# A hybrid encoder layer on one core: query scaling in the scan's first level, eleven low weight parts made and stored beside the last input pairs, and the order of steps around them

## The chip, the cores and the metric

The kernel runs on one core of a Trainium2 chip. The metric is the device time of one execution in microseconds (us). Before the change three executions took 1735.74, 1736.81 and 1737.69 us; the median is 1736.81 us. A profile of one more execution, which took 1736.41 us, is the source of every duration below.

## The reference

For one sequence of 1024 positions and 1024 channels, the layer computes

```python
h = rmsnorm(x)
glu_in, q, v, z_f, z_b, og, g_a, g_b = split(h @ w_in)        # 1024 x 8192
a = pointwise(silu(layernorm(dwconv31(glu(glu_in)))))
o = scan(q, k_f, v, f_f) + flip(scan(flip(q), flip(k_b), flip(v), flip(f_b)))   # 8 heads of 128
b = (rmsnorm(o) * silu(og)) @ o_w
x = x + (sigmoid(g_a) * a + sigmoid(g_b) * b) @ w_out
h2 = rmsnorm(x)
x = x + (silu(dwconv3(h2 @ w_gate)) * (h2 @ w_up)) @ w_down
out = rmsnorm(x)
```

`scan` is a gated linear recurrence per head, S_t = diag(f_t) S_(t-1) + k_t v_t', o_t = S_t' q_t, with the forget gate f and the key k = (1 - lb) sigmoid(-z), where lb is a learned bound per channel and direction. Everything is float32.

## The kernel before, in words

**Dense products.** Every weight tile is cut into a high part (an ACT cast, L125) and a low part (a VectorE subtract, L125), and every product is three TensorE matmuls (L149, L150, L151: low activation times high weight and so on) of 128x128 by 128x512. The program writes TensorE's order by hand: a job yields after each *piece*, and `fill(n)` on a stream makes the next n pieces of it (fractions are owed). What VectorE, ACT, GpSimd (POOL) and the DMA queues do is placed around that by a scheduler; `pin` holds an instruction where it was written.

**Input pairs.** The columns of `w_in` are taken two tiles at a time, 19 pairs (`in_pair`), each by seven products of half-size blocks (84 dense matmuls). Of each pair VectorE makes weight sums and low parts (`wq`, `wp`, and for some pairs the sums `sw` and `wr` at L298; for the other pairs POOL's accumulating DMAs make those sums), and combines the products as they end (`ev`, L800). TensorE reuses a few PSUM banks here (`tr`, `mm`, `sc`), so a later product waits until the `ev` of an earlier one has read its bank.

**Conv stage, about 100 to 340 us.** `conv_steps` makes the 31 taps of four channel tiles on VectorE (L1036, L1039: 128x1024 multiply-add, 124 of them); after each tap `s_pairs.fill(CONV_FILL)` puts in 1.67 pieces of the input pairs.

**LayerNorm stage, about 400 to 470 us.** For each half of the sequence: the mean by a matmul with `ones_m` (L1065), subtraction (L1067), squares on ACT, their sum (`tm`, L1051 and L1053) into a matmul (L611), the scale, then normalise, SiLU and split (L1077 to L1082). Pieces of the last pairs lie between: six after the mean, five after the sum of squares, twelve at the end of a half.

**Scan stage, about 510 to 865 us.** There are 16 half-heads. `scan_base` (L1220) prepares one: scaled keys, products of queries and forget gates, and running products of gates by doubling (L1144); its fourth step has TensorE's first group of small matmuls (called S here: `sc<-q,A` and `sc<-A,A`, L1195). `scan_levels` (L1280) goes on with two more levels (called O: `ob<-A,A`, L1195), sixteen zero matmuls that clear a bank (L1302), `blocks(32)` and `blocks(64)` (L1281, called B32 and B64); `scan_states` has the transposes of the keys (L1320) and the state updates (L1329); `scan_outputs` (L1370) follows a head later, fed by `pending`. Between these steps `between` puts in 1.77 pieces of dense filler (`std_job` columns of `w_in`), one step of the next half-head's base, and one step of pending outputs. The filler's low parts are made by VectorE as each tile arrives.

**End.** The last dense jobs leave the final rows (`final_evac`, `turn_out`, `finish`): transposes at L1890 and the scale on ACT at L1926.

## Time and profile before

| what | value |
|---|---|
| profiled execution, its own time | 1736.41 us |
| its span in the profile | 1734.3 us (2.1 us lie outside it) |
| median of three unprofiled runs | 1736.81 us |
| TensorE (PE) busy | 1709.2 us, 99% |
| VectorE (DVE) busy | 1255.9 us, 72% |
| ScalarE (ACT) busy | 830.3 us, 48% |
| GpSimd (POOL) busy | 170.4 us, 10% |
| granted TensorE clock | 0.998 |

A busy share counts from the start of a matmul to its modelled end, so overlapped matmuls hide small gaps: for TensorE the distance from one start to the next says more. Where TensorE waits, the table of waits names the instruction that waited, the engine and line that released it, the sum, the number of such waits and the longest.

### The profile page before, as it was taken

How to read it: one execution, taken by the hardware profiler on the slowest of the kernel's cores; microseconds unless marked ns; L12 is line 12 of the kernel's file. 1: busy time of each engine (PE TensorE's matmuls, PEld its weight loads, DVE VectorE, ACT ScalarE, POOL GpSimd, SP SyncE). 2: the span in 40 equal slices, each digit the busy share in tenths (PEclk: the TensorE clock that was granted, in tenths of full speed). 3: DMA queues.
4: the chain of work that ended last, by engine and by line, in shares of the span. 5: the costliest groups of instructions: out<-in, count | busy, mean ns of one | idle time of the engine just before them, and what ended most of it. 6: DMA issues, size and time to landing. Idle time of an engine off the chain costs nothing.

```text
span 1734.3 us, 30669 instructions
## 1 busy us (share of the span) xinstructions
PE 1709.2 (99%) x11902; PEld 1415.0 (82%) x11902; DVE 1255.9 (72%) x1937; ACT 830.3 (48%) x1544; POOL 170.4 (10%) x185
## 2 busy tenths in 40 slices
PE   8999999999999999999999999999999999999997
PEld 6878888888788888888878888888888888888787
DVE  5599999746778888888557466667767776657865
ACT  7444443334566777776442245444434433542334
POOL 2211111100000000000000002011111111000110
PEclk9999999999999999999999999999999999999999
DMA  8768888854673444435579466568777776783842
GB/s 288 239 167 184 193 194 193 197 167 154 207 230 104 131 126 132 127 115 192 175 248 333 147 207 205 146 148 170 158 170 160 180 172 153 229 267 107 205 91 98
DMA packets 343751, 308.27 MB, mean 178 GB/s; under 512 B 25262, under 2 KB 255798, under 8 KB 343606
## 3 DMA queue, kind: packets, MB, share of 16 engines
q1 hardware_dynamic: 289590, 267.51, 48.7%
q0 software_dynamic: 44800, 37.76, 15.2%
q10 hardware_dynamic: 9216, 1.05, 0.4%
q8 instruction: 93, 1.52, 0.4%
q14 instruction: 52, 0.43, 0.1%
HBM read 201.40 MB, written 87.03 MB: 166 GB/s over the span
## 4 chain that ended last, share of the span: by engine, by line
PE 44%; DMA 2%; DVE 2%; ACT 1%; issue 1%; SPq 0%; POOL 0%; POOLq 0%; ACTq 0%; DVEq 0%
PE mm L151 10%; PE mm L150 10%; PE mm L149 10%; PE sc L149 3%; PE sc L150 3%; PE sc L151 3%; PE tr L149 1%; PE tr L150 1%; PE tr L151 1%; DMA tm<-d_bm 1%; DVE hx L125 0%; DMA wr<-in_ffn_w_down_dram 0%; DMA wr<-wr 0%; DMA d_gc<-ft 0%; DVE wp L125 0%
## 5 line engine op out<-in xcount | busy, mean ns | idle before, releaser
L149 PE MATMUL mm<-hx,wp 128*128 128x512 f32 x1068 | 428.0, 401 | 3.3 <-ACT tm L851 2.1
L151 PE MATMUL mm<-hx,wp 128*128 128x512 f32 x1068 | 418.1, 391 | 0.9 <-DVE wp L125 0.8
L150 PE MATMUL mm<-hx,wp 128*128 128x512 f32 x1068 | 416.9, 390 | 0.3 <-DVE hx L125 0.2
L125 ACT CAST wp<-wr 128x1024 fp32r<-128x1024 f32 (+2 forms) x147 | 147.2, 1002 | 259.2 <-PE mm L150 119.5
L151 PEld LDWEIGHTS mm<-hx,wp 128*128 128x128 f32 x1068 | 200.9, 188 | 46.3 <-DVE wp L125 3.4
L149 PEld LDWEIGHTS mm<-hx,wp 128*128 128x128 f32 x1068 | 200.8, 188 | 46.1 <-ACT tm L851 2.6
L150 PEld LDWEIGHTS mm<-hx,wp 128*128 128x128 f32 x1068 | 201.2, 188 | 41.3 <-DVE hx L125 1.6
L125 DVE TENSOR_TENSOR wp<-wr,wp 128x1024 fp32r<-128x1024 f32 (+2 forms) x145 | 169.3, 1168 | 68.5 <-ACT wp L125 67.9
L1039 DVE SCALAR_TENSOR_TENSOR acc<-gl,v_b,acc 128x1024 f32<-128x1024 f32 x120 | 148.9, 1277 | 0.4
L1144 DVE TENSOR_TENSOR qF<-qF,tb 128x512 f32<-128x512 f32 x96 | 65.0, 684 | 20.8 <-ACT A L1176 20.7
L440 ACT COPY su<-mm 128x512 f32<-128x512 f32 x82 | 47.7, 582 | 66.2 <-PE mm L151 66.2
L149 PE MATMUL tr<-hx,wp 128*128 128x512 f32 x180 | 70.5, 392 | 0.0
L125 ACT CAST wq<-sw 128x1024 fp32r<-128x1024 f32 x41 | 43.2, 1053 | 56.3 <-PE mm L150 40.5
L151 PE MATMUL tr<-hx,wp 128*128 128x512 f32 x180 | 70.1, 389 | 0.0
L150 PE MATMUL tr<-hx,wp 128*128 128x512 f32 x180 | 70.0, 389 | 0.0
L1636 DVE SCALAR_TENSOR_TENSOR tm<-gp,v_a,tm 128x512 f32<-128x512 f32 x88 | 65.9, 749 | 3.9 <-ACT tm L1634 2.0
L1144 DVE TENSOR_TENSOR kG<-kG,tb 128x512 f32<-128x512 f32 x96 | 65.1, 684 | 3.7 <-PE sc L1281 3.7
L149 PE MATMUL mm<-hy,wp 128*128 128x512 f32 x164 | 64.2, 391 | 0.0
L149 PE MATMUL sc<-hy,wq 128*128 128x512 f32 x164 | 64.2, 391 | 0.0
L151 PE MATMUL sc<-hy,wq 128*128 128x512 f32 x164 | 63.8, 389 | 0.0
L150 PE MATMUL mm<-hy,wp 128*128 128x512 f32 x164 | 63.8, 389 | 0.0
L150 PE MATMUL sc<-hy,wq 128*128 128x512 f32 x164 | 63.8, 389 | 0.0
(372 smaller groups left out, 3609.9 us busy)
## 6 DMA issues: line engine op xcount, KB each, us to landing
wr<-in_w_in_dram SPq DMA_DIRECT2D x48, 512.0 KB
wr<-in_ffn_w_up_dram SPq DMA_DIRECT2D x22, 512.0 KB
sw<-in_w_in_dram SPq DMA_DIRECT2D x38, 256.0 KB
d_g<-ft SPq DMA_DIRECT2D x38, 256.0 KB
sw<-in_ffn_w_up_dram SPq DMA_DIRECT2D x38, 256.0 KB
sw<-in_ffn_w_up_dram POOLq DMA_DIRECT2D x19, 512.0 KB, 8.1
wr<-sw POOLq DMA_DIRECT2D x32, 256.0 KB, 3.8
wr<-wr POOLq DMA_DIRECT2D x32, 256.0 KB, 4.1
```

What stands on the lines that cost most here:

```text
L125: parts = A.copy(hi, src), eng.tensor_tensor(lo, src, hi.bitcast(F32), op=ALU.subtract)
L149: T.matmul(acc, whi[:, k, :], ahi, start=first, stop=False, skip_group_check=again)
L150: T.matmul(acc, whi[:, k, :], alo, start=False, stop=False, skip_group_check=again)
L151: T.matmul(acc, wlo[:, k, :], ahi, start=False, stop=last, skip_group_check=again)
L440: A.copy(t, acc)
L1039: V.scalar_tensor_tensor(acc, g[:, k : k + S], tap(k), acc, op0=ALU.mult, op1=ALU.add)
L1144: V.tensor_tensor(o, a, b, op=op)
L1636: V.scalar_tensor_tensor(c, g[:, o + k : o + k + H], vec("fdw", k * NF + j), c, op0=ALU.mult, op1=ALU.add,)
```

## The change

It has seven parts.

1. `CONV_FILL` goes from 1.67 to 1.6, so 124 taps carry 198 pieces instead of 207.
2. `first` holds from pair 12 on instead of 14: pairs 12 and 13 make their weight sums on VectorE and no longer by POOL's accumulating DMAs.
3. `low_part`: for eleven filler tiles of the scan (the fourth to the fourteenth), POOL loads the raw tile (512 KB) in the LayerNorm stage, five pieces later ACT casts it and VectorE subtracts (both pinned), and two pieces later POOL stores the result. One tile is begun every five pieces. In the scan these tiles' low parts are loaded by the SP queue; VectorE makes none for them.
4. In the LayerNorm stage the twelve pieces at the end of a half become 1.5 pieces after each of the four channel tiles and 1.5 at the end.
5. In `scan_base` the keys are no longer scaled in place; the scale goes into the sum of keys and into the queries' first products (two 128x512 and four 128x256 instructions in place of three 128x512 sums and products and two scalings).
6. In `scan_levels` the zero matmuls and B32 come straight behind O, and two fills instead of one lie before B64. The next base is begun two steps earlier (its first step falls into the half-head before), and in `between` the base's step comes behind `pending`.
7. At the end the transposes of the final rows come a few pieces later.

TensorE gets the same matmuls in another order (7757 rows before and after). VectorE has 1853 rows before and 1843 after, ACT 1396 and 1389, POOL 184 and 200, SP 891 and 904.

**VectorE, conv stage, third pair** (`acc` a tap; `ev` from `tr`, `mm`, `sc` the combining of the products; `wq` from `sw` and from `w` two low parts). Before:

```order
L800 TENSOR_TENSOR ev_1873<-tr_1818,su_1833 128x512
L1039 SCALAR_TENSOR_TENSOR acc_1532<-gl_473,v_b,acc_1532 128x1024
L1039 SCALAR_TENSOR_TENSOR acc_2057<-gl_464,v_b,acc_2057 128x1024
L1039 SCALAR_TENSOR_TENSOR acc_1532<-gl_473,v_b,acc_1532 128x1024
L1039 SCALAR_TENSOR_TENSOR acc_2057<-gl_464,v_b,acc_2057 128x1024
L1039 SCALAR_TENSOR_TENSOR acc_1532<-gl_473,v_b,acc_1532 128x1024
L800 TENSOR_TENSOR ev_1921<-su_1906,mm_1817 128x512
L125 TENSOR_TENSOR wq_1863<-sw_1850,wq_1862 128x1024
L1039 SCALAR_TENSOR_TENSOR acc_1532<-gl_473,v_b,acc_1532 128x1024
L125 TENSOR_TENSOR wq_1870<-w_302_1860,wq_1870 128x512
```

After, the same place:

```order
L1045 SCALAR_TENSOR_TENSOR acc_1543<-gl_484,v_b,acc_1543 128x1024
L806 TENSOR_TENSOR ev_1885<-tr_1830,su_1845 128x512
L1045 SCALAR_TENSOR_TENSOR acc_1543<-gl_484,v_b,acc_1543 128x1024
L1045 SCALAR_TENSOR_TENSOR acc_2054<-gl_475,v_b,acc_2054 128x1024
L1045 SCALAR_TENSOR_TENSOR acc_1543<-gl_484,v_b,acc_1543 128x1024
L1045 SCALAR_TENSOR_TENSOR acc_2054<-gl_475,v_b,acc_2054 128x1024
L1045 SCALAR_TENSOR_TENSOR acc_1543<-gl_484,v_b,acc_1543 128x1024
L125 TENSOR_TENSOR wq_1875<-sw_1862,wq_1874 128x1024
L1045 SCALAR_TENSOR_TENSOR acc_1543<-gl_484,v_b,acc_1543 128x1024
L125 TENSOR_TENSOR wq_1882<-w_302_1872,wq_1882 128x512
L806 TENSOR_TENSOR ev_1933<-su_1918,mm_1829 128x512
```

One tap moved ahead of the first `ev`, and both low parts and a tap moved ahead of the `ev` that frees the bank `mm`.

**VectorE, LayerNorm, second half**, from the subtraction of the mean to the last `tm` before the sum of squares (`sw` and `wr` at L298 are weight sums). Before:

```order
L1067 SCALAR_TENSOR_TENSOR cx_3969<-ob_4022,cx_3969 128x512 x2
L1067 SCALAR_TENSOR_TENSOR cx_3972<-ob_4022,cx_3972 128x512 x2
L298 TENSOR_TENSOR wr_4032<-wr_4032,sw_4034 128x512
L1051 TENSOR_TENSOR tm_4102<-tm_4102,tm_4103 128x512
L298 TENSOR_TENSOR wr_4032<-wr_4032 128x512
L1053 TENSOR_TENSOR tm_4102<-tm_4102,tm_4104 128x512
L1053 TENSOR_TENSOR tm_4102<-tm_4102,tm_4105 128x512
```

After (`lw` at L1076 is a new low part; the first of its subtractions of `cx`, the same row with `cx_3925`, is left out above the first row):

```order
L1095 SCALAR_TENSOR_TENSOR cx_3928<-ob_4007,cx_3928 128x512 x2
L125 TENSOR_TENSOR wq_3954<-sw_3939,wq_3953 128x1024
L806 TENSOR_TENSOR ev_4028<-su_3999,mm_3896 128x512
L806 TENSOR_TENSOR ev_4044<-sc_3898,su_3984 128x512
L125 TENSOR_TENSOR wq_3961<-w_621_3951,wq_3961 128x512
L1076 TENSOR_TENSOR lw_3975<-lw_3885,lw_3975 128x1024
L1057 TENSOR_TENSOR tm_4076<-tm_4076,tm_4077 128x512
L303 TENSOR_TENSOR sw_4120<-sw_4120,sw_4123 128x1024
L1076 TENSOR_TENSOR lw_4025<-lw_3973,lw_4025 128x1024
L125 TENSOR_TENSOR wp_3958<-wr_3937,wp_3957 128x1024
L1059 TENSOR_TENSOR tm_4076<-tm_4076,tm_4078 128x512
L1059 TENSOR_TENSOR tm_4076<-tm_4076,tm_4079 128x512
```

Between the mean and the last `tm` two wr rows became two `lw`, two `wq`, two `ev`, a `wp` and the sum `sw`, which needs a load.

**TensorE, scan, first half-head**: O (`ob<-A,A`), the zero matmuls (`none`, sixteen of them, the first shown) and dense matmuls (`hx,wp`). Before:

```order
L151 MATMUL mm_4640<-hx_4311,wp_4450 128x512
L1195 MATMUL ob_4674<-A_4577,A_4575 32x32 x16
L1195 MATMUL ob_4674<-A_4623,A_4621 32x32 x16
L149 MATMUL mm_4640<-hx_4317,wp_4449 128x512
L150 MATMUL mm_4640<-hx_4318,wp_4449 128x512
L151 MATMUL mm_4640<-hx_4317,wp_4450 128x512
L149 MATMUL mm_4640<-hx_4323,wp_4449 128x512
L150 MATMUL mm_4640<-hx_4324,wp_4449 128x512
L151 MATMUL mm_4640<-hx_4323,wp_4450 128x512
L1302 LDWEIGHTS none
L1302 MATMUL sc_4730<-none 32x32
```

After, up to the first zero matmul, and then from the last one on (`qF,kG` 32x32 is B32, `ident,tm` the transposes of v):

```order
L151 MATMUL mm_4722<-hx_4392,wp_4532 128x512
L1228 MATMUL ob_4772<-A_4659,A_4657 32x32 x16
L1228 MATMUL ob_4772<-A_4705,A_4703 32x32 x16
L1336 LDWEIGHTS none
L1336 MATMUL sc_4805<-none 32x32
```

```order
L1336 MATMUL sc_4805<-none 32x32
L1318 MATMUL sc_4805<-qF_4504,kG_4417 32x32 x16
L149 MATMUL mm_4722<-hx_4398,wp_4531 128x512
L150 MATMUL mm_4722<-hx_4399,wp_4531 128x512
L151 MATMUL mm_4722<-hx_4398,wp_4532 128x512
L149 MATMUL mm_4722<-hx_4404,wp_4531 128x512
L150 MATMUL mm_4722<-hx_4405,wp_4531 128x512
L151 MATMUL mm_4722<-hx_4404,wp_4532 128x512
L1509 MATMUL tr_4862<-ident,tm_4770 128x128 x4
```

The six dense matmuls moved from between O and the zero matmuls to behind B32, ahead of the transposes.

The diff, cut to its core:

```diff
@@ -19,16 +19,16 @@
 TAIL = ((1, 2), (1, 1), (2, 4), (2, 3))
-CONV_FILL = 1.67
+CONV_FILL = 1.6
 NPAIRS = 19
+STAGE_FROM, STAGED, STAGE_STEP = 3, 11, 5
 LN_FILL = 6
-LN_LAST = 12
+LN_STEP = 1.5
 GLU_FIRST = 4
...
 GLU_LATE = 17
-BASE_STEPS = 1
 ALIGN = 128
...
 EPS = 1e-6

@@ -248,12 +248,17 @@
-    def std_job(src, nk, acts, evac, halves=(0, 1), step=2):
+    def std_job(src, nk, acts, evac, halves=(0, 1), step=2, low=None):
...
             raw = raw_w(src, nk)
-            return split(w_page(nk), w_page(nk), raw, V)
+            if low is None:
+                return split(w_page(nk), w_page(nk), raw, V)
+            hi, lo = w_page(nk), w_page(nk)
+            nc.sync.dma_start(lo.bitcast(F32), low)
+            A.copy(hi, raw)
+            return hi, lo
...
             for half in halves:

@@ -563,6 +568,7 @@
     d_z = scratch("d_z", 2, NH, 2)
+    d_lo = [dp.tile([P, ND, P], F32, name=f"d_lo_{i}") for i in range(STAGED)]
     d_bm = scratch("d_bm", NH, 2)
...
     d_xt = [[d_x0[:, :, k, :], scratch(f"d_xt_{k}")] for k in range(ND)]

@@ -838,7 +844,7 @@
             lambda e, *quadrant: evs[e](*quadrant),
-            first=n == 0 or n >= 14,
+            first=n == 0 or n >= 12,
             columns=2,
...

@@ -1053,6 +1059,28 @@
+    def low_part(i):
+        src = in_cols(todo[2 * NPAIRS + STAGE_FROM + i][0])
+        def w_tile(dt):
+            return gp0.tile([P, ND, P], dt, tag="gl", name=nm("lw"), bufs=NCW)
+        def fetch_raw():
+            raw = w_tile(F32)
+            G.dma_start(raw, src)
+            later(5, lambda: take(raw))
+        def take(raw):
+            lo = w_tile(F32R)
+            pin(A.copy(lo, raw))
+            pin(V.tensor_tensor(lo, raw, lo.bitcast(F32), op=ALU.subtract))
+            later(2, lambda: G.dma_start(d_lo[i], lo.bitcast(F32)))
+        later(1 + STAGE_STEP * i, fetch_raw)
+    for i in range(STAGED):
+        low_part(i)
     for half in range(2):
...
         for j in range(NCW):

@@ -1077,17 +1105,22 @@
             A.activation(xn, xn, AF.Silu)
+            s_pairs.fill(LN_STEP)
             both = gp0.tile([P, 2, H], F32R, tag="gl", name=nm("ch"), bufs=NCW)
...
                 nc.sync.dma_start(dst, part.bitcast(F32))
-        s_pairs.fill(LN_LAST)
+            s_pairs.fill(LN_STEP)
     s_pairs.drain()
...
     rest = todo[2 * NPAIRS :]
-    rest_jobs = [std_job(in_cols(c), ND, h_std, e) for c, e in rest[:-2]]
+    lows = [None] * STAGE_FROM + d_lo
+    rest_jobs = [
+        std_job(in_cols(c), ND, h_std, e, low=lo)
+        for (c, e), lo in itertools.zip_longest(rest[:-2], lows[: len(rest) - 2])
+    ]
     (c0, e0), (c1, e1) = rest[-2:]
...
     ca = [[None, None] for _ in range(NCW)]

@@ -1220,22 +1253,26 @@
         D_t = hp.tile([P, 4, 32], F32, tag="D", name=nm("D"), bufs=3)
-        for d in range(2):
-            V.tensor_scalar(kG[:, d, :], kG[:, d, :], ks[:, d : d + 1], None, op0=ALU.mult)
         k_d, Q1 = page(hp, "A", 8), page(hp, "A", 8)
-        tt(k_d, kG[:, 0, :], kG[:, 1, :], ALU.add)
+        V.tensor_scalar(k_d, kG[:, 1, :], ks[:, 1:2], None, op0=ALU.mult)
+        V.scalar_tensor_tensor(k_d, kG[:, 0, :], ks[:, 0:1], k_d, op0=ALU.mult, op1=ALU.add)
         A1 = woven(kG, 1)
         odd = H // 2
-        tt(
-            pairs(Q1, 1, 0),
-            view(q, 0, [[1, 2], [2, odd], [1, 1]]),
-            view(f, H, [[1 - H, 2], [2, odd], [1, 1]]),
-        )
-        tt(
-            view(qF, 1, [[H - 1, 2], [2, odd]]),
-            view(q, 1, [[-1, 2], [2, odd]]),
-            view(f, H + 1, [[-(H + 1), 2], [2, odd]]),
-        )
+        def gated(to, at, t, d):
+            V.scalar_tensor_tensor(
+                view(to, at, [[2, odd]]),
+                view(q, t, [[2, odd]]),
+                ks[:, d : d + 1],
+                view(f, d * H + t, [[2, odd]]),
+                op0=ALU.mult,
+                op1=ALU.mult,
+            )
+        for t in range(2):
+            gated(Q1, t, t, 1 - t)
+        for t in (1, 0):
+            gated(qF, (1 - t) * H + t, t, t)
         double_keys(kG, f, 1)
...
         tb = totals(f, 1)

@@ -1294,15 +1331,16 @@
         level(slot(b, 1), A16, row(Q16))
+        S_b = bank("sc")
+        for at, g, _ in each():
+            T.matmul(S_b[g, at : at + 32], none, none, start=True, stop=True)
+        blocks(S_b, 32)
         for n, m in enumerate((m_8, m_16)):
             V.copy_predicated(D_t, over(m), near(slot(b, n)))
-        yield
-        b = bank("sc")
-        for at, g, _ in each():
-            T.matmul(b[g, at : at + 32], none, none, start=True, stop=True)
-        blocks(b, 32)
         tb = double(tb, 32)
         yield
+        yield
+        b = S_b
         blocks(b, 64)
...
         A.copy(S_t, c4(b))

@@ -1438,11 +1476,12 @@
     cur = Base(scan_inputs(0))
-    ins = scan_inputs(1)
+    ahead = Base(scan_inputs(1))
     dense.fill(7)
...
         dense.fill(pieces)
+    ahead.step(1)
     pending = Stream(iter(()))
...
         Tt = hp.tile([P, 2, 2, 4], F32, tag="Tt", name=nm("Tt"), bufs=4)

@@ -1452,14 +1491,14 @@
             base = cur.result()
-            ahead = Base(ins) if i + 1 < NI else None
-            ins = scan_inputs(i + 2) if i + 2 < NI else None
-            def between(fill):
-                dense.fill(fill)
-                if ahead is not None:
-                    ahead.step(BASE_STEPS)
+            following = Base(scan_inputs(i + 2)) if i + 2 < NI else None
+            def between(n):
+                dense.fill(FILL)
                 pending.fill(1)
+                step_of = ahead if n < 4 else following
+                if step_of is not None:
+                    step_of.step(1)
...
             vl = load(d_v[h][half])

@@ -1470,12 +1509,12 @@
                     A.copy(v.rearrange("p c e -> p (c e)"), b)
-                between(FILL)
+                between(n)
             qF, kG = base[:2]
-            for _ in scan_states(i, kG, v, Tt, Sf, Sb):
-                between(FILL)
+            for n, _ in enumerate(scan_states(i, kG, v, Tt, Sf, Sb)):
+                between(3 + n)
             kept.append((S_t, v, qF))
-            cur = ahead
+            cur, ahead = ahead, following
         pending = Stream(outputs(h, kept, Tt, Sf, Sb))
...
     dense.owed = 0

@@ -1877,7 +1916,7 @@
         V.tensor_tensor(t, acc, t, op=ALU.add)
-        later(4, lambda: turn_out(i, half, chunks))
+        later(8 - len(chunks), lambda: turn_out(i, half, chunks))
...

@@ -1998,8 +2037,8 @@
     for n, part in enumerate(PARTS[:-1]):
-        st.fill(4 * ND * (n + 1) + 3 - st.count)
-        finish(*part, late=2 + 2 * n)
+        st.fill(4 * ND * (n + 1) + (3, 5)[n] - st.count)
+        finish(*part, late=6)
     st.drain()
...
     finish(*PARTS[-1], late=0)
```

## The prediction

> **What bounds the kernel now.** I read the page first: the engines' busy shares.
>
> ```profile
> PE 1709.2 (99%) x11902; PEld 1415.0 (82%) x11902; DVE 1255.9 (72%) x1937; ACT 830.3 (48%) x1544; POOL 170.4 (10%) x185
> ```
>
> TensorE is the bound, and its matmul count does not change. So only two things can move the time: stalls of TensorE, and the distance between matmuls of different shapes. The table of waits gives the first.
>
> ```profile
> PE sc L1281 <- DVE qF L1144: 2.0, 2, 1.0
> PE sc L1890 <- ACT y L1926: 1.5, 1, 1.5
> PE mm L149 <- DVE ev L800: 0.8, 1, 0.8
> PE mm L149 <- ACT su L440: 0.7, 1, 0.7
> PE sc L1329 <- ACT kT L1322: 0.3, 1, 0.3
> ```
>
> These are the waits at the places that the change touches: 5.3 us in all. The table of windows tells which engine stands close behind in each stage (columns: TensorE, weight loads, VectorE, ACT, POOL busy).
>
> ```profile
> 150.00:200.00 50.00, 50.00 (x222) 41.41 (x221) 49.91 (x49) 20.56 (x30) 8.50 (x8) 1.00 0.89 202
> 400.00:450.00 50.00, 49.26 (x217) 39.83 (x217) 33.73 (x47) 22.93 (x38) 1.23 (x2) 1.00 0.64 206
> 600.00:700.00 100.00, 98.87 (x1568) 83.31 (x1567) 82.79 (x182) 72.19 (x164) 3.68 (x4) 1.00 0.39 120
> ```
>
> In the conv stage VectorE has no air at all (49.91 of 50). In the LayerNorm stage it has a third free, in the scan a sixth. All sums below are made against the profiled execution, 1736.41 us; the median, 1736.81, is 0.4 higher, which is too little to correct for.
>
> **Conv stage (`CONV_FILL` 1.6): later by 2.8 us.** First VectorE, then TensorE, in the third pair.
>
> ```profile
> 161.79 6.06 DVE L1039 SCALAR_TENSOR_TENSOR acc<-gl,v_b,acc 128x1024 f32<-128x1024 f32 x5
> 167.77 0.68 DVE L800 TENSOR_TENSOR ev<-su,mm 128x512 f32<-128x512 f32 x1
> 168.37 1.22 DVE L125 TENSOR_TENSOR wq<-sw,wq 128x1024 fp32r<-128x1024 f32 x1
> 169.50 1.28 DVE L1039 SCALAR_TENSOR_TENSOR acc<-gl,v_b,acc 128x1024 f32<-128x1024 f32 x1
> 170.72 0.69 DVE L125 TENSOR_TENSOR wq<-w,wq 128x512 fp32r<-128x512 f32 x1
> ```
>
> ```profile
> 169.87 0.39 PE L149 MATMUL mm<-hx,wp 128*128 128x512 f32 x1
> ```
>
> From start to start a tap takes 1.20 us (five from 161.79 to 167.77), a long low part 1.13, a short row 0.60. The matmul at 169.87 takes over the bank `mm`, so it needs the `ev` that starts at 167.77 and ends at 168.45: 1.42 us to spare. In the new order a tap comes ahead of the first `ev`, and the long low part, a tap and the short one come ahead of this `ev`: 1.20 + 1.13 + 1.20 + 0.60 = 4.1 us later on an engine without air. That is a stall of 4.1 - 1.4 = 2.7 us. Counting the rows of both orders on in the same way, the same `ev` stands 4.7 us later in the seventh pair, and there the spare is smaller:
>
> ```profile
> 241.70 0.81 DVE L1036 TENSOR_SCALAR acc<-gl,v_b,v_a 128x1024 f32<-128x1024 f32 x1 [1.16 <-DMA d_cv<-acc]
> 244.82 0.68 DVE L800 TENSOR_TENSOR ev<-su,mm 128x512 f32<-128x512 f32 x1
> ```
>
> ```profile
> 246.03 0.39 PE L149 MATMUL mm<-hx,wp 128*128 128x512 f32 x1
> ```
>
> Here 246.03 - 245.50 = 0.53 us are spare, so TensorE must be 4.2 us late by then, less some tenths if the 1.16 us for which VectorE waits for a store shrink: I take 4.0. Later pairs ask for no more. In the kernel before, this stage had its own stalls on the same `ev` at 304 and 323 us, 0.9 and 0.3 (the longer one is the row of 0.8 in the waits), and a TensorE that is already 4 us late meets neither: 4.0 - 1.2 = 2.8 (1.5 to 3.3). `first` from pair 12 adds three sums on VectorE in each of two pairs, 2 x (1.13 + 2 x 0.60), after 340 us; its cover is the free third there, and where it stands in the way it is counted next.
>
> **LayerNorm stage: later by 5.3 us (2.5 to 9.5).** The measure is the first half in the trace.
>
> ```profile
> 407.68 2.48 DVE L1067 SCALAR_TENSOR_TENSOR cx<-ob,cx 128x512 f32<-128x512 f32 x4 [1.21 <-PE ob L1065]
> 420.29 1.23 DVE L125 TENSOR_TENSOR wq<-sw,wq 128x1024 fp32r<-128x1024 f32 x1 [1.39 <-ACT wq L125]
> 425.97 1.23 DVE L298 TENSOR_TENSOR sw<-sw,sw 128x1024 f32<-128x1024 f32 x1 [3.26 <-DMA sw<-in_w_in_dram]
> ```
>
> ```profile
> 415.66 0.95 PE L611 MATMUL ob<-ones_m,tm 128*128 128x1 f32 x8
> ```
>
> From the subtraction of the mean to the matmul on the sum of squares TensorE has 415.66 - 407.68 = 8.0 us of dense work. In the first half of the new order VectorE has 8.3 us of rows there: two long ones (2.3) and ten short (6.0); with ACT's squares in the chain I take 0.6 us of stall. In the second half it has five long rows and ten short, 5 x 1.13 + 10 x 0.60 = 11.7 us. One of the long ones, `sw`, needs a load that can start when the `wq` before it has read its page; in the trace that takes from 421.5 to 425.9, 4.4 us, and only 3.5 us of other rows lie between. So 11.7 + 0.9 - 8.0 = 4.6 us, or 3.7 without the load: I take 4.1. While VectorE stands there, the `tm` behind it stand, and TensorE behind them.
>
> The third place is the end of the stage, where ACT's pinned casts of the last low parts wait for their raw loads on POOL's queue, with the copies that free TensorE's banks (`su`, L440) behind them.
>
> ```profile
> sw<-in_w_in_dram POOLq DMA_DIRECT2D x13, 512.0 KB, 8.6
> wr<-wr POOLq DMA_DIRECT2D x32, 256.0 KB, 4.1
> ```
>
> In the new order the last of these loads is issued about 16 matmuls ahead of its cast, 16 x 0.227 = 3.6 us. No row shows a plain 512 KB load on that queue; the nearest are 8.6 us (512 KB, accumulating) and twice 4.1 us, and from below the 4.4 us of the SP load. The wait is thus 0.8 to 5 us, of which the spare of a bank, 1.4 us as at 169.87, may hide a part: I take 1.5 (0 to 4). [...]
>
> Against these three stands the `su` wait of 0.9 us at 436 (0.7 in the table), which goes since the casts of the four channel tiles are spread: 0.6 + 4.1 + 1.5 - 0.9 = 5.3.
>
> **Scan: earlier by 7.5 us (4.5 to 10).** Two pieces of TensorE's row, each start to be compared with the next.
>
> ```profile
> 643.74 0.76 PE L1195 MATMUL ob<-A,A 128*32 128x32 f32 x64
> 644.43 0.50 PE L149 MATMUL mm<-hx,wp 128*128 128x512 f32 x1
> 644.76 0.39 PE L150 MATMUL mm<-hx,wp 128*128 128x512 f32 x1
> ```
>
> Four more dense ones on:
>
> ```profile
> 645.69 0.40 PE L151 MATMUL mm<-hx,wp 128*128 128x512 f32 x1
> 646.01 0.28 PE L1302 MATMUL sc<-none 128*32 128x32 bf16 x16
> 646.13 0.47 PE L1281 MATMUL sc<-qF,kG 128*32 128x32 f32 x32
> 646.52 0.66 PE L1470 MATMUL tr<-ident,tm 128*128 128x128 f32 x4
> ```
>
> ```profile
> 652.00 0.39 PE L1370 MATMUL ob<-Sb,qF 128*128 128x128 f32 x2
> 652.32 0.69 PE L1281 MATMUL sc<-qF,kG 128*64 128x64 f32 x16
> ```
>
> And twelve dense ones on:
>
> ```profile
> 655.90 0.46 PE L1195 MATMUL sc<-q,A 128*32 128x32 f32 x32
> 656.17 1.18 PE L1195 MATMUL sc<-A,A 128*32 128x32 f32 x96
> 657.31 0.46 PE L1370 MATMUL ob<-v,S 128*128 128x128 f32 x2
> 657.61 0.39 PE L1370 MATMUL ob<-Sf,qF 128*128 128x128 f32 x2
> ```
>
> Dense matmuls follow each other at 0.23 us. Entering a small group costs 0.32 - 0.23 = 0.09 (645.69 to 646.01). Small matmuls among small ones take 0.27 / 32 = 8.4 ns (655.90 to 656.17); O took 0.69 for 64, so leaving it cost 0.15, and B32 0.39 for 32, 0.12. The first dense one behind is late again, 0.33 for 0.23: 0.10. Zero matmuls to B32 cost nothing (0.12 for 16).
>
> Before, O out and back, then zero matmuls and B32 out and back: 0.09 + 0.15 + 0.10 + 0.09 + 0.12 = 0.55 a half-head. After, one such trip: 0.09 + 0.12 + 0.10, and 0 to 0.09 into the transposes that now follow dense work: 0.35. Saved 0.20. For S and B64: before, B64 was entered from an output group (652.00 to 652.32, 0.10 above the 0.22 of these), S from dense work (0.09), and left into outputs (0.12, and 0.08 at 657.31): 0.39. After, S is entered at 0.09 and B64 follows directly, which no row shows: 0 at best, 0.22 if it is an exit and an entry. I take 0.13, nearer to a change of form than to none: 0.22, saved 0.17. Then 16 x 0.37 = 5.9 us (3.5 to 8). [...]
>
> The waits of B64 (2.0) and of the state update (0.3) go: two fills, 12 dense matmuls or 2.7 us, now lie where one lay, and the wait is 1.0 at its longest. I set 0.7 against it (0 to 2), since B32 now stands a fill earlier and the base's step comes behind the outputs. The net is -5.9 - 2.3 + 0.7 = -7.5.
>
> Scaling the queries costs nothing. The nearest rows:
>
> ```profile
> L1224 DVE TENSOR_SCALAR kG<-kG,kscale 128x512 f32<-128x512 f32 x26 | 12.5, 481 | 13.5 <-ACT kG L1163 13.3
> L1144 DVE TENSOR_TENSOR tb<-tb 128x256 f32<-128x256 f32 x14 | 5.9, 421 | 0.1
> ```
>
> Removed are 2 x 0.48 and three rows of about 0.69, added 0.48 + 0.6 + 4 x 0.42: 3.0 and 2.8 us. The eleven low parts no longer made here free 11 x 1.2 us of VectorE, hidden anyway behind dense work; their loads on SP have 15 to 20 us ahead of the first use, against 4.4 needed.
>
> **End: earlier by 1.5.** The wait for `y` goes with the later transposes (0.5 to 1.5). **Sum:** 1736.4 + 2.8 + 5.3 - 7.5 - 1.5 = 1735.5.
>
> **The rivals.**
> *A, the stalls stay hidden and the scan gives its full amount.* VectorE may run its rows of the last pairs ahead of the mean, and ACT's chain may be short. Conv +1.5, LayerNorm +2.5, scan -10, end -1.5: 1728.9. For it: a third of VectorE is free at 400 to 450. Against: the order on an engine is fixed.
> *B, the POOL queue decides, slower.* Raw loads, stores and pages share one queue and four pages; if a load takes more than the 3.6 us of lead by the full 5, and the casts of earlier low parts wait too, ACT holds the banks: LayerNorm +9.5, scan -5, conv +2.8, end -1.5: 1742.2. It decides as soon as loads take over 5.0 us (3.6 + 1.4).
> *C, the change does not do in the scan what it says.* If each group pays its own weight change whatever its neighbour, only the waits go, -2: 1741.0.
>
> **How the numbers follow.** Forecast 0.36 (own range 1733 to 1739.5), A 0.34 (1727 to 1733), B 0.18 (1740.5 to 1746), C 0.12 (1739.5 to 1742). The range 1728.5 to 1742.5 leaves out a tenth on each side. A measurement here tells about 0.2%, 3.5 us, from no change: faster means under 1733.3 and slower over 1740.3. Faster: A and a little of the forecast's lower edge, 0.38. Slower: B and most of C, 0.28. Within: 0.34.
>
> **What would show it.** Right: a wait of `mm` for `ev` of about 2.7 us near 170, one at L611's successor of 4 us in the second half of LayerNorm, waits behind `lw` at the stage's end, no wait at B64, and O, zero matmuls and B32 in one block of about 1.1 us. Wrong: no waits between 160 and 480, or dense groups in the scan that still open with 0.33 as often as before.

## The result, and the profile after

The changed kernel took **1762.95 us** (median of 4 runs, 1756.41 to 1766.13), the kernel before 1737.25 (4 runs, 1735.74 to 1739.19): ratio **1.014** (95%: 1.0122 to 1.0158). The forecast was 1735.5 with a range of 1728.5 to 1742.5, so it was wrong, by 27 us, and outside even the slower rival's 1742.2. The profiled execution took 1765.0 us (span 1763.2, mean granted clock 0.992 where it was 0.998).

To place the difference, take matmuls that have the same work ahead of them in both orders, and read when they start (us from the span's start):

| kernel | 1400th dense matmul (end of conv) | first small group of the scan | last output group of the scan | span |
|---|---|---|---|---|
| before | 346.8 | 504.4 | 873.3 | 1734.3 |
| after | 357.0 | 534.2 | 904.7 | 1763.2 |
| difference of the stage | +10.2 | +19.6 | +1.6 | -2.5 |
| forecast | +2.8 | +5.3 | -7.5 | -1.5 |

The signs are right but for the scan. Two stages lost far more than forecast, and the scan gained nothing. First the page's busy line and the largest rows of the table of waits for TensorE, after (columns: us in total, times, longest):

```profile
PE 1713.4 (97%) x11902; PEld 1419.6 (81%) x11902; DVE 1265.0 (72%) x1959; ACT 835.3 (47%) x1555; POOL 180.2 (10%) x201
```

```profile
PE ob L1093 <- DVE tm L1059: 6.4, 1, 6.4
PE mm L149 <- DVE ev L806: 6.0, 4, 2.6
PE ob L617 <- DVE tm L1059: 4.9, 2, 4.4
PE tr L1358 <- DVE kG L1177: 3.8, 4, 1.9
PE mm L149 <- ACT su L445: 2.7, 3, 1.3
...
PE sc L1367 <- ACT kT L1360: 2.1, 3, 1.0
```

The waits for `qF` at B64 and for `y` at the end are gone, as forecast, and `ev` and L617 stand where they were forecast. The longest of all, the mean of the second half (`ob` L1093), was in no term of the sum, and two waits of the scan (`kG`, `kT`) are new or longer. The 2.6 us of `ev` is the one worked out beforehand, in VectorE's row:

```profile
169.49 1.22 DVE L125 TENSOR_TENSOR wq<-sw,wq 128x1024 fp32r<-128x1024 f32 x1
170.63 1.28 DVE L1045 SCALAR_TENSOR_TENSOR acc<-gl,v_b,acc 128x1024 f32<-128x1024 f32 x1
171.82 0.69 DVE L125 TENSOR_TENSOR wq<-w,wq 128x512 fp32r<-128x512 f32 x1
172.42 0.68 DVE L806 TENSOR_TENSOR ev<-su,mm 128x512 f32<-128x512 f32 x1
```

```profile
173.16 0.50 PE L149 MATMUL mm<-hx,wp 128*128 128x512 f32 x1 [2.61 <-DVE ev L806]
...
174.77 0.63 PE L151 MATMUL mm<-hx,wp 128*128 128x512 f32 x1
```

The `ev` now follows both low parts and a tap, and the matmul at 173.16 waits for it. But look at the next row: 1.6 us later a matmul of the same shape lasts 0.63 us, not 0.39. The table of windows says why (after; behind the engines' busy times stand the granted clock, where 1.00 is full speed, the DMA share and GB/s):

```profile
174.00:177.50 3.50, 3.50 (x10) 2.72 (x9) 3.29 (x4) 0.63 (x1) 1.58 (x1) 0.51 0.64 222
...
436.00:455.00 19.00, 13.99 (x61) 10.97 (x59) 9.96 (x13) 5.74 (x9) 2.85 (x4) 0.97 1.00 334
458.50:461.00 2.50, 2.50 (x7) 1.98 (x7) 2.48 (x4) 0.97 (x2) 0.00 (x0) 0.56 0.43 160
...
472.50:477.50 5.00, 5.00 (x16) 4.32 (x17) 1.33 (x2) 0.62 (x3) 2.82 (x3) 0.50 0.82 231
```

From 174.0 to 177.5 us, beginning 0.8 us behind the end of the wait, the granted clock is 0.51 and dense matmuls follow each other at 0.43 us: a wait of 2.6 us costs 1.6 us more. The same stands behind the mean (458.50 to 461.00, 0.56) and behind the 4.4 us at L617 (472.50 to 477.50, 0.50). From 436 to 455 us the DMA engines are busy all the time (share 1.00), and that is where VectorE waits for LayerNorm's own input:

```profile
446.48 0.69 DVE L1057 TENSOR_TENSOR tm<-cx 128x512 f32<-128x512 f32 x1 [3.28 <-DMA cx<-d_cv]
...
454.46 0.69 DVE L1059 TENSOR_TENSOR tm<-tm,cx 128x512 f32<-128x512 f32 x1 [1.48 <-DMA cx<-d_cv]
...
455.67 0.69 DVE L1059 TENSOR_TENSOR tm<-tm,cx 128x512 f32<-128x512 f32 x1
```

```profile
456.41 2.08 PE L1093 MATMUL ob<-tm,ones_m 128*128 128x512 f32 x2 [6.42 <-DVE tm L1059]
```

The `cx` load feeds the sum `tm`, the sum feeds the mean, and TensorE stands 6.42 us. The DMA issues between 425 and 462 us (KB each, median us from issue to landing), after:

```profile
lw<-in_w_in_dram POOLq DMA_DIRECT2D x4, 512.0 KB, 6.9
...
cx<-d_cv SPq DMA_DIRECT2D x4, 256.0 KB, 10.8
```

Without staging (experiment e1, same window) it is 3.7. Of the four `cx` loads each trace has the landing of one only, so each of these figures is one load:

```profile
cx<-d_cv SPq DMA_DIRECT2D x4, 256.0 KB, 3.7
```

So the staged tiles do not only wait for themselves, as the prediction had it: they make another queue's loads late. The first half has a smaller copy of it, on the `ev` rows, and there it is a store that is held up. First SP's queue, then VectorE:

```profile
338.52 4.05 SPq L1050 DMA_DIRECT2D d_cv<-acc  x1
...
346.34 0.80 SPq L1089 DMA_DIRECT2D cx<-d_cv  x2
```

```profile
348.73 0.69 DVE L1059 TENSOR_TENSOR tm<-tm,cx 128x512 f32<-128x512 f32 x1 [6.78 <-DMA cx<-d_cv]
...
350.47 0.68 DVE L806 TENSOR_TENSOR ev<-su,mm 128x512 f32<-128x512 f32 x1
```

The store of the last taps takes 4.05 us to issue, beside the raw load that POOL issued at 334.2; in e1 it takes 0.57. `cx` reads back what that store wrote, so it is issued at 346.34. VectorE stands 6.78 us before a `tm` that needs `cx`, and goes on at 348.73. It stands 6.22 there in the kernel before too, where TensorE meets no wait, and 3.67 in e1; here the `ev` queued behind it comes too late, TensorE waits 2.0 us for it, and 1.7 us of half clock follow. This lies ahead of the 1400th dense matmul and counts in the +10.2.

Two things are told wrongly above. The 1.5 pieces stand twice in each channel tile's loop (behind the SiLU and behind the split), eight times 1.5 in a half: the twelve pieces are spread over the whole loop. And the first three raw loads are not in the LayerNorm stage: POOL issues them at 188, 238 and 334 us, as soon as pages come free; only casts and stores wait for it.

### The profile page after: what moved, and what is told of

Read it like the earlier page. It is cut to its first block, busy times and chain, and to the rows that moved or that the text cites. A ratio compares the mean times of both kernels' runs of the same rounds, so it can differ in the third digit from the quotient of the medians.

```text
span 1763.2 us, 30773 instructions
## 1 busy us (share of the span) xinstructions
PE 1713.4 (97%) x11902; PEld 1419.6 (81%) x11902; DVE 1265.0 (72%) x1959; ACT 835.3 (47%) x1555; POOL 180.2 (10%) x201
## 5 line engine op out<-in xcount | busy, mean ns | idle before, releaser
L125 ACT CAST wp<-wr 128x1024 fp32r<-128x1024 f32 (+2 forms) x136 | 135.7, 999 | 259.1 <-PE mm L150 109.5
L125 DVE TENSOR_TENSOR wp<-wr,wp 128x1024 fp32r<-128x1024 f32 (+2 forms) x134 | 156.1, 1166 | 65.5 <-ACT wp L125 59.0
```

Of the source, the lines that this page charges most:

```text
L125: parts = A.copy(hi, src), eng.tensor_tensor(lo, src, hi.bitcast(F32), op=ALU.subtract)
```

## The experiments

My theories at the outset were three: *staging* (the transfers of the eleven low parts make the LayerNorm stage late), *fill* (the twelve pieces, spread out, leave too little work ahead of the second mean), and *order* (the scan's new order makes its own waits). Later came *transfer* against *engine work* inside staging, *queue*, and *clock*.

| run | median us (range) | before on that chip | ratio (95%) | conv end | first small group | last output group |
|---|---|---|---|---|---|---|
| e1_stage0 | 1743.51 (1741.42–1750.03) | 1738.43 | 1.003 (1.0014–1.0046) | 351.9 | 508.9 | 881.2 |
| e2_lnlast | 1764.1 (1759.94–1766.73) | 1738.43 | 1.0139 (1.0111–1.0166) | 352.7 | 528.7 | 898.1 |
| e3_fill167 | 1761.47 (1756.08–1763.78) | 1738.43 | 1.0121 (1.0092–1.0151) | 346.8 | 518.0 | 899.1 |
| e4_scan | 1741.13 (1737.24–1742.91) | 1738.43 | 1.0011 (0.9998–1.0025) | 346.7 | 504.4 | 875.8 |
| e5_dmaonly | 1765.03 (1761.12–1768.81) | 1739.21 | 1.0147 (1.0119–1.0175) | 361.9 | 529.6 | 901.3 |
| e7_busy | 1761.46 (one execution) | 1739.21 | none | | | |
| e8_levels_tail | 1731.98 (1731.02–1733.05) | 1739.21 | 0.9955 (0.9937–0.9973) | 345.2 | 502.7 | 868.8 |
| e9_shift | 1735.83 (1733.62–1737.81) | 1739.21 | 0.9979 (0.9967–0.999) | 345.3 | 502.7 | 873.0 |
| e10_loads | 1755.06 (1753.23–1757.02) | 1737.77 | 1.009 (1.0071–1.0109) | 356.4 | 520.8 | 893.1 |
| e12_spq | 1752.94 (1751.87–1755.46) | 1737.77 | 1.0079 (1.0061–1.0098) | 354.3 | 520.6 | 890.3 |
| e11_best_q | 1735.32 (1733.07–1739.52) | 1737.77 | 0.9981 (0.9969–0.9993) | 345.0 | 502.5 | 870.4 |
| e6_q | 1737.6 (1734.38–1742.25) | 1739.95 | 0.9986 (0.9974–0.9998) | 345.0 | 502.7 | 872.4 |

The last three columns are starts in one trace each, as in the table above. A conv end of some 345 instead of 347 is a difference from around 97 us, where these kernels are alike; the last section tells its cause. e2, e3 and e12 have the same lead of 1.8 to 1.9 us over the kernel before, so their conv stages lost that much more than the column says.

**e1_stage0: the change without staging.**

```diff
-STAGE_FROM, STAGED, STAGE_STEP = 3, 11, 5
+STAGE_FROM, STAGED, STAGE_STEP = 3, 0, 5
```

> The changed kernel without the eleven staged low parts (the scan's filler makes them on VectorE again). Changed kernel: 1763 us. Staging theory (the staged loads, stores, casts and subtractions are what stops TensorE in the LayerNorm stage, by a full DMA and VectorE's extra rows): 14 to 19 us of the LayerNorm stage's loss go, 1744 to 1749. Fill theory (the twelve pieces at a half's end, now spread, leave too little dense work ahead of the second mean): at most 5 go, 1758 to 1763.

It gave 19.4 us back (1762.95 to 1743.51). From the end of conv to the scan it takes 508.9 - 351.9 = 157.0 us, no more than before (157.6). TensorE's waits between 100 and 500 us:

```profile
PE mm L149 <- DVE ev L806: 3.0, 3, 2.6
```

Only the forecast stall near 170 is left; the waits at the mean, at L617 and for `su` have gone, all of them. So all that the LayerNorm stage lost needs staging. What stays is conv's 5.1 us (the stall and its half clock in the main) and 3.4 us in the scan.

**e2_lnlast: the twelve pieces back at a half's end.**

```diff
             A.activation(xn, xn, AF.Silu)
-            s_pairs.fill(LN_STEP)
...
-            s_pairs.fill(LN_STEP)
+        s_pairs.fill(12)
```

> The changed kernel with the twelve pieces of LayerNorm back at the end of each half, staging kept. Fill theory: the wait of 6.4 us at the second mean goes, with the slow matmuls behind it, 8 to 12 us less, 1751 to 1755. Staging theory: the loads are late all the same and VectorE's rows stay, 0 to 4 us less, 1759 to 1763.

```profile
PE ob L617 <- DVE tm L1059: 6.0, 2, 5.5
PE mm L149 <- DVE ev L806: 5.8, 5, 3.6
PE ob L1093 <- DVE tm L1059: 1.8, 1, 1.8
```

```profile
cx<-d_cv SPq DMA_DIRECT2D x4, 256.0 KB, 5.6
```

The mean's wait falls from 6.4 to 1.8, as the fill theory has it, but the waits at L617 (6.0 for 4.9), the longest `ev` (3.6 for 2.6, in the conv stage) and the `su` wait at the stage's end (3.4 for 1.2) grow, and the time stays (1.0139 beside 1.014). The `cx` load takes 5.6 us here. The fill theory falls as an explanation of the time.

**e3_fill167: `CONV_FILL` back.**

```diff
-CONV_FILL = 1.6
+CONV_FILL = 1.67
```

> The changed kernel with CONV_FILL back at 1.67. Order theory (the rows ahead of the combining of products on a VectorE without air make the whole loss of 10 us between 140 and 350): that loss goes, 1752 to 1755, and no wait for that row is over 1 us. Rival (staging that starts in the conv stage, or the extra sums of pairs 12 and 13, make a part): 2 to 6 us go, 1757 to 1761.

```profile
PE ob L1093 <- DVE tm L1059: 7.0, 1, 7.0
PE mm L149 <- DVE ev L806: 2.8, 3, 1.1
```

Conv ends at 346.8 as before, and no `ev` wait exceeds 1.1: the 2.6 us stall of conv is made by this number alone. (1.9 us of that agreement are the lead from 97 us, so the stage still loses 1.9, with two waits of 1.1 in it.) But the total hardly moves, against what I expected. The stages behind give it back: at the scan's start a group waits 3.6 and again 1.6 us for ACT's `A`, the granted clock is 0.54 from 524 to 531 us, and the scan takes 381.1 us, 12.2 more than before. What conv saves is thus lost again behind it, where staging is late; that its longer conv stage had served as slack is the reading, not a thing shown.

**e4_scan: before, with the new order of the scan alone** (`scan_levels` and the loop that begins the bases; diff as in part 6 of the change, without the query scaling).

> The kernel before with the new scan order alone (zero matmuls and B32 behind O, two fills ahead of B64, the next base two steps earlier); keys scaled as before, no staging. In the changed kernel the scan lost 1.5 us against before. Order theory (neighbouring small matmuls save about 6 us, and waits of the key transposes and state updates, made by the order itself, eat 8): 1736 to 1740. Rival (those waits come from the other parts, the query scaling or the low parts' loads): 6 to 8 us faster, 1729 to 1731.

```profile
PE tr L1321 <- DVE kG L1144: 5.4, 4, 2.5
PE sc L1195 <- ACT A L1176: 1.6, 2, 1.4
PE sc L1330 <- ACT kT L1323: 1.0, 2, 0.6
```

The scan takes 371.4 us instead of 368.9, with no staging anywhere: the order makes its own waits, and they are those of the changed kernel. The waits sum to 8.0 us where before they were 2.3, and behind two of them (2.5 us at 588 and 2.1 at 724) the clock falls to half as well (mean granted clock 0.995 where before has 0.998); the stage is only 2.5 longer, so the transitions are saved all the same, and the waits eat them.

**e5_dmaonly: staging's transfers without its engine work.** The raw tile is stored in place of a low part (so the scan multiplies by raw weights where low parts belong); casts and subtractions are left out.

```diff
-            lo = w_tile(F32R)
-            pin(A.copy(lo, raw))
-            pin(V.tensor_tensor(lo, raw, lo.bitcast(F32), op=ALU.subtract))
-            later(2, lambda: G.dma_start(d_lo[i], lo.bitcast(F32)))
+            later(2, lambda: G.dma_start(d_lo[i], raw))
```

> The changed kernel with the staging's transfers alone: the raw tile is loaded and stored as it came, the casts and subtractions are left out (so the scan's filler multiplies by the raw tile in place of its low part). Without any staging it was 1743.5 us, with all of it 1763 on the first chip. Transfer theory (POOL's loads and stores fill the DMA engines, so that LayerNorm's own loads come late, with slow matmuls behind the waits): at least 10 of the 19.5 us stay, 1754 to 1760. Row theory (VectorE's and ACT's extra rows ahead of the rows that TensorE waits for): at most 6 stay, 1744 to 1750.

The whole loss stays (1.0147) with eleven fewer casts and subtractions, so a loss of this size does not need the engine work. It does not fall in the same places: without casts to wait for, four loads and stores go between 187 and 228 us and cost there (conv end 361.9), and LayerNorm loses 10.1 instead of 19.6, with 9.2 at the mean.

**e7_busy: 24 extra matmuls ahead of the second mean**, into its own bank, which the mean overwrites.

```diff
+        if half:
+            part = ht[1][0][0]
+            for _ in range(24):
+                T.matmul(mean, part[:, :P], part, start=True, stop=True)
         T.matmul(mean, ones_m, total(xs, tmp()), start=True, stop=True)
```

> The changed kernel with 24 extra dense matmuls ahead of the second half's mean matmul, into the bank that it overwrites, so that TensorE computes through most of its wait of 6.4 us there. Clock theory (a wait of 2 us or more is followed by about 3.5 us at half the granted clock, 1.5 us lost each time): the granted clock stays at 1.0 behind the mean matmul, the slow matmuls there go, and the mean matmul itself starts no later. Rival (the matmuls are slow because their operands are late or the memories are busy): they are as slow as before.

```profile
446.49 5.60 PE L1096 MATMUL ob<-hx 128*128 128x512 f32 x24
```

```profile
452.50:456.50 4.00, 4.00 (x17) 2.99 (x16) 3.18 (x5) 2.45 (x4) 0.00 (x0) 1.00 0.81 244
```

Where TensorE waited in the changed kernel it now works, and the clock behind the mean is 1.00 where it was 0.56. The mean itself comes no later for it. So the half clock at this place is the price of the idle time, not of the transfers that caused it: they go on, at a DMA share of 0.81. One execution, 1761.46, lies inside the changed kernel's own range and says nothing of the total.

**e8_levels_tail: before, with the new `scan_levels` (zero matmuls and B32 behind O, two fills ahead of B64) and the later transposes of the end; loop and bases as before.**

```diff
+        S_b = bank("sc")
+        for at, g, _ in each():
+            T.matmul(S_b[g, at : at + 32], none, none, start=True, stop=True)
+        blocks(S_b, 32)
...
-        later(4, lambda: turn_out(i, half, chunks))
+        later(8 - len(chunks), lambda: turn_out(i, half, chunks))
```

> The kernel before with two parts of the change: in the scan's levels the zero matmuls and B32 behind O and two fills ahead of B64, but the next base as before (so S stays between B64 and the key transposes), and the end's transposes later. Cover theory (the new waits for key transposes came from moving S ahead of B64): no wait of over 0.5 us at the key transposes, none at B64, scan loss 4 to 5 us below before, the end 1.5 below: 5 to 6.5 us faster than before. Rival (O and B32 in one block alone bring the waits): within 1.5 us of before.

```profile
640.84 0.75 PE L1195 MATMUL ob<-A,A 128*32 128x32 f32 x63
...
641.41 0.30 PE L1299 MATMUL sc<-none 128*32 128x32 bf16 x15
641.54 0.52 PE L1281 MATMUL sc<-qF,kG 128*32 128x32 f32 x32
641.99 0.50 PE L149 MATMUL mm<-hx,wp 128*128 128x512 f32 x1
```

```profile
PE ob L1371 <- DVE Sb L1423: 1.7, 2, 1.2
PE sc L1330 <- ACT kT L1323: 0.6, 1, 0.6
```

From O's start to the first dense matmul behind B32 it is 1.15 us, the one block that was foretold (1.1). The `qF` wait at B64 is gone; 2.3 us of other waits came, the same sum as in the kernel before. The scan takes 366.1 us, 2.8 less than before, close to the 16 x 0.20 = 3.2 that this part of the sum gave. **This version beats both kernels** (0.9955, 0.9937 to 0.9973). Of the 5.0 us between the two spans the table puts 2.8 into the scan and 0.5 behind it; 1.7 lie at the very beginning, in work that the edit does not touch. The medians lie 7.2 apart, and one trace of each does not place the rest.

**e9_shift: e4 with 1.5 pieces moved from behind B32 to between B64 and the transposes of the keys.**

```diff
-                dense.fill(FILL)
+                dense.fill(FILL + (-1.5, 0, 1.5, 0, 0)[n])
```

> The new scan order alone with 1.5 pieces moved from behind B32 to between B64 and the key transposes. With the scan order alone the waits of the key transposes were 5.4 us in four places, and the time 1741.1. Cover theory: 3 to 5 us of these waits go, 1736 to 1738. Rival (VectorE is simply late by its work in those half-heads, wherever the dense matmuls lie): they come back at another place, 1740 to 1742.

```profile
PE sc L1195 <- ACT A L1176: 5.2, 6, 1.5
```

The `kG` waits of e4 (5.4 us) are gone, so what was missing there was cover between B64 and the transposes. But the waits as a whole are not fewer: those for `A` grow from 1.6 to 5.2, 2.7 us come for which the profile names no releaser, and the sum is 9.0 where e4 had 8.0. So the waits come back at another place, as the rival had it, while the time is that of the cover theory: the ratio is 0.9979 where e4 had 1.0011. The scan takes 370.3 us against 371.4, and only a fifth of that difference lies in the scan of these two traces. What moves the waits is shown; a saving in the scan is not.

**e10_loads: of staging only the raw loads** (nothing is made of them; the scan makes its low parts as before).

```diff
-            later(5, lambda: take(raw))
...
-    lows = [None] * STAGE_FROM + d_lo
+    lows = [None] * len(d_lo)
```

> The changed kernel with the staging's raw loads alone: eleven loads of 512 KB on POOL's queue, nothing made of them and nothing stored; the scan's filler makes its low parts itself. Without staging the loss against before was 7 us, with all of it 29. Transfer theory, by bytes: half the staged bytes of these stages, so 10 to 18 us of loss, 1748 to 1757. Page theory (it is the stores and the waits for pages, not the bytes, that hold others up): within 3 us of the kernel without staging, 1741 to 1747.

```profile
lw<-in_w_in_dram POOLq DMA_DIRECT2D x4, 512.0 KB, 8.7
cx<-d_cv SPq DMA_DIRECT2D x4, 256.0 KB, 11.5
```

The loads alone, 5.8 MB of which nothing is used, make `cx` as late as the whole of staging does (11.5 beside 10.8) and TensorE wait 5.2 us at the mean. They cost 1755.06 - 1743.51 = 11.5 us over e1, more than half of staging's 19.4; each figure is against its own chip, and by the ratios it is 1.009 against 1.003, 10 us.

**e12_spq: staging's loads and stores on SP's queue.**

```diff
-            G.dma_start(raw, src)
+            nc.sync.dma_start(raw, src)
...
-            later(2, lambda: G.dma_start(d_lo[i], lo.bitcast(F32)))
+            later(2, lambda: nc.sync.dma_start(d_lo[i], lo.bitcast(F32)))
```

> The changed kernel with the staged loads and stores on SP's queue in place of POOL's. Byte theory (the DMA engines are full, whichever queue issues): 1755 to 1766. Queue theory (POOL's queue takes turns away from SP's, whose loads LayerNorm waits for): the transfers keep their order on SP's queue, and at least 8 us of the loss go, 1745 to 1755.

```profile
cx<-d_cv SPq DMA_DIRECT2D x4, 256.0 KB, 5.1
```

```profile
PE mm L149 <- DVE ev L806: 10.3, 4, 4.4
PE ob L1093 <- DVE tm L1059: 1.1, 1, 1.1
```

The same bytes on the queue that carries `cx` itself: the `cx` load lands in 5.1 us, the mean's wait falls to 1.1, and 10 us of the loss are gone (1.0079 against 1.014). It is no cure: the `ev` behind VectorE's other late inputs now waits 4.4. And whether the queue did it is not shown, since the order changed with it. In e12 a staged load and a store (issued at 434.1 and 437.9 us) stand ahead of the four `cx` loads (438.4 to 440.6), and the next staged load behind them (443.4). In the changed kernel a store and a load of 512 KB (442.9 and 443.4) were issued less than 1 us ahead of the third `cx` load (443.6), the one that took 10.8. In e2, on POOL's queue, nothing staged was issued in the 5 us ahead of the last `cx` load, and that one took 5.6. So it may be what is in flight at that moment; the queue by itself is not singled out.

The changed kernel also issues its last two `cx` loads later, 87 and 88 us behind the end of conv, where e1 and e10 have 79 and 80. That alone costs little: e12 issues them at 86 and the mean waits 1.1 us, while e10, which issues them as early as e1, waits 5.2.

**e6_q and e11_best_q: the query scaling alone, on before and on e8** (part 5 of the change).

> The kernel before with the query scaling alone (keys unscaled, the scale in the sum of keys and in the queries' first products). Forecast's step (it costs nothing): within 2 us of before, scan loss within 1 us of before. Rival (its rows stand on VectorE ahead of what the state updates and key transposes wait for, as the fast version with it, 1735.3 against 1732.0 without, hints): 2 to 5 us slower, with longer waits at those places.

> The fast version (zero matmuls and B32 behind O, two fills ahead of B64, the later transposes at the end: 1732.0 us) with the query scaling as well. If the scaling costs nothing, as forecast: within 1.5 us of 1732. Rival (it adds to VectorE's work ahead of S, so that S waits for its operands): 2 to 5 us slower, 1734 to 1737.

The rows of e6 (busy us, mean ns):

```profile
L1230 DVE SCALAR_TENSOR_TENSOR A<-q,kscale,f 128x256 f32<-128x256 f32 x30 | 13.3, 481 | 0.0
L1225 DVE SCALAR_TENSOR_TENSOR A<-kG,kscale,A 128x512 f32<-128x512 f32 x15 | 11.2, 746 | 0.0
```

A half-head costs 0.48 + 0.75 + 4 x 0.48 = 3.15 us of VectorE for the 3.0 removed, and on before the ratio is 0.9986 (95%: 0.9974 to 0.9998). On e8 the run is slower than e8 was, 1735.32 beside 1731.98, on another chip; its scan takes 367.9 us against 366.1, with 2.7 instead of 1.7 us of waits for `Sb` (the rival of that run had named S). A cost of 1.8 us, as the two scans have it, to 3.3, as the medians have it, is possible and not settled.

## Why the prediction was wrong

**Conv, +10.2 for 2.8.** The step itself held: 2.7 us were worked out for the `ev` in the third pair, the profile shows 2.6, and e3 shows that `CONV_FILL` alone makes it. Two things were left out. The half clock behind the stall costs 1.6; it could be seen in the trace of before, where it stands at 99 us, and I took a dense matmul at 0.23 us everywhere. And the first half's `cx` load, issued late behind a store that ran beside a staged load, gives a second `ev` wait of 2.0 and 1.7 us of half clock behind it; both are gone in e1. The third omission is smaller: I let one 4 us delay cover all later pairs, but four stalls of 0.2 to 0.9 us between 251 and 311 us came as well, 2.2 in all.

**LayerNorm, +19.6 for 5.3: the step that failed.** Each of the three terms came out near its size: 0.6 foretold for the first sum of squares, 0.5 seen; 4.1 for the second, 4.4 seen; 1.5 for the `su` at the stage's end, 1.2 seen. The credit of 0.9 for another `su` wait was not given, since one of 1.3 came at 422 us. The step on the casts held too: ACT waits 3.4 us for the last raw load, and the `su` behind it is what TensorE waits for.

```profile
505.22 1.05 ACT L1075 CAST lw<-lw 128x1024 fp32r<-128x1024 f32 x1 [3.41 <-DMA lw<-in_w_in_dram]
```

What failed is that the sum 0.6 + 4.1 + 1.5 - 0.9 = 5.3 stops there: it priced a staged transfer only by the instruction that waits for that same transfer, and put its effect on all other loads at nothing, without a reason. What the runs show in its place is a wait of 6.4 us at the second mean, and a half clock behind it and behind L617 of some 2.1 and 2.6 us (against the same rows at full clock in e7 and e1). With the stage's other waits, less the 0.7 that the kernel before had, these make 18 of the 19.6. The mean waits because `cx`, on SP's queue, is late: one load takes 10.8 us where e1 has 3.7; e10 gets 11.5 with loads of which nothing is used; e5 keeps the whole loss without the casts. The prediction quoted a DMA share of 0.64 for 400 to 450 us, an average; the same trace has 0.90 from 425 to 445 and 0.98 from 430 to 438, so there was little room at this place.

The 4.4 at L617 was right partly by luck. Without the two `lw` rows the same count still leaves 4.1 - 2 x 1.13 = 1.8 us, and e1 shows no wait there. Nor does the traffic alone make it: e5 and e10 have it without the `lw` rows, and no wait at L617 either. How much belongs to the rows and how much to late inputs stays open.

**Scan, +1.6 for -7.5.** The transitions were right where they could be measured alone (e8: 2.8 of the 3.2). In the changed kernel TensorE's stalls in the scan (starts at least 0.2 us later than the usual distance) add up to 11.3 us beside the 2.8 of before, and the stage is 1.6 longer, so about 11.3 - 2.8 - 1.6 = 6.9 us of transitions were saved, where 5.9 were forecast. The waits at B64 went. The step that failed is "I set 0.7 against it (0 to 2)". B64 now follows S without dense work between, VectorE's last doubling needs B64's read to be over, and the transposes of the keys need that doubling: what had been covered by S is open. e4 shows these waits without any other part of the change (5.4 for `kG`, 1.6 for `A`, 1.0 for `kT`); e8, which has the new `scan_levels` but the old loop, so that S still lies between B64 and the transposes, shows none for `kG`; and e9 shows the missing cover, since the 5.4 us for `kG` go when 1.5 pieces are moved there, though as much comes back as other waits. The sentence in the prediction named the new neighbour, and its price was taken from a wait that had already been paid for, not from the rows of the new chain.

**End, -2.5 for -1.5.** The `y` wait is gone. Among the kernels with the old end (before, e4, e6, e9) the stretch behind the scan takes 861.0 to 864.0 us, among those with the new one 858.5 to 862.0, so the size is not sharper than 2 us.

**Rival B** looked at the right queue, and put the price at the wrong place: the casts that wait for POOL's loads, with 9.5 for the whole stage. **A** and **C** are out: the stalls were not hidden, and e8 shows the scan's saving.

## What to carry to other kernels

A transfer is not priced by its own consumer alone: where the DMA share is near 1 (here 1.00 from 436 to 455 us), list every load that lands in the same stretch on any queue, and ask which engine waits first if each takes three times as long (here 10.8 us for 3.7). When a group is moved in a hand-written order, ask what it had been covering where it stood. A wait of TensorE is worth more than its length where the clock falls behind it (here by 1.4 to 2.6 us), so look for that in the trace of before and put it into each forecast stall.

## What the runs showed of the hardware that was not expected

**Waits of some 2 us had the half clock behind them at some places and not at others.** All fourteen traces have the same wait at 97 us, ahead of the same matmuls. In seven it lasts 1.9 to 2.5 us, and each time 7 or 8 matmuls at 0.43 us follow and cost 1.4 to 1.6; in the other seven it lasts 1.4 to 1.8, and none follows. First the row of before (wait 2.1), then that of e8 (wait 1.6), granted clock 0.50 and 1.00:

```profile
99.00:102.00 3.00, 3.00 (x9) 2.32 (x8) 3.00 (x6) 1.59 (x3) 0.74 (x5) 0.50 0.15 49
```

```profile
98.50:101.50 3.00, 3.00 (x15) 2.49 (x14) 3.00 (x6) 1.65 (x3) 0.74 (x5) 1.00 0.39 131
```

That is the 1.5 to 2 us by which some kernels are ahead at the end of conv. The half clock lasts no longer there: 8 x 0.43 = 3.4 us, and in the trace of before the matmuls from 102.27 on follow each other at 0.23 to 0.24 again. At other places a wait of about this length had both outcomes. One wait of 2.0 us stands at the same place in e5 (552 us) and in the changed kernel (557 us); behind it the clock was 0.53 in e5 and 1.00 in the changed kernel:

```profile
552.50:556.00 3.50, 3.50 (x14) 2.96 (x14) 2.02 (x5) 0.59 (x1) 0.00 (x0) 0.53 0.19 43
```

```profile
557.00:560.00 3.00, 3.00 (x18) 2.55 (x18) 2.13 (x6) 1.24 (x3) 0.00 (x0) 1.00 0.28 61
```

In the traces of the kernel before and of the changed one, from 90 to 1700 us, the half clock stands behind the waits of 1.95 us (at 351), 2.14 and 2.53 (both at 97), 2.61, 4.44 and 6.42, and behind no other; the longest of the others are 1.87 (at 755) and 1.99 (at 557).

**A 256 KB load on SP's queue took 3.7 us without staged transfers (e1), and 8.2 to 11.5 where two or three 512 KB transfers had been issued on POOL's queue in the 5 us ahead of it.** These are one load of each trace: e3 8.2, e7 9.9, the changed kernel 10.8, e5 11.4, e10 11.5. In e2, with none issued so close ahead, it took 5.6. The 512 KB loads themselves took 6.9 in the changed kernel and 8.7 in e10 (medians of four), where the lead given to them was 3.6.

**Open:** whether e12 gained by the queue or by the order that came with it; what the 2.0 us are that TensorE loses at 557 us with no releaser in the profile, and in four other kernels with staged low parts (0.4 to 2.2 us); and what decides, beside the length, whether a 2 us wait halves the clock.
